# Attention projections of a two-layer float32 trunk: panels in pairs, four row tiles of each pair in seven block products, head norms scaled on ScalarE

## The chip, the cores and the metric

The kernel runs on one core of one Trainium2 chip. The metric is the device time of one execution in microseconds; the kernel before has a median of 2073.8 us over three runs.

## The reference

Everything is float32; 256 tokens, width 2048, 16 heads of 128, hidden width 8192, two layers. Cut to what matters:

```python
# layer a
u = rms_norm(h, a_norm_g)
q, k, v, fz = split(u @ a_w_in, [D, 2*D, 3*D])      # a_w_in: 2048 x (3*2048 + 16)
q, k = rms_norm per head (a_q_g, a_k_g)
logf = log_sigmoid(fz + a_b_f); c = cumsum(logf)
s = q k^T / sqrt(128) + c[query] - c[key], causal; p = softmax(s); o = p v
h = h + o @ a_w_out
h = h + relu(rms_norm(h, g) @ w1)**2 @ w2           # w1: 2048 x 8192
# shared keys and values, once
k_sh, v_sh = split(rms_norm(h, kv_norm_g) @ kv_w, [D]); k_sh = rms_norm per head
# layer b
q = rms_norm per head (rms_norm(h, b_norm_g) @ b_w_q)
s = q k_sh^T / sqrt(128) + relative-position bias, chunks of 64 masked; p = softmax(s)
h = h + (p v_sh) @ b_w_out
h = h + relu(rms_norm(h, g) @ w1)**2 @ w2
```

## The kernel before

**Products.** The 256 tokens are two blocks of 128 (`NB`), the width is 16 row tiles of 128 (`KT`). An output of 512 columns is a *panel*; its accumulators are two tiles of 128 x 512, one for each block of tokens. Activations lie on chip with the width on partitions, in two parts, `hi` and `lo`, and so does every weight tile while it is used; a float32 product is the sum of three passes, hi by hi, lo by hi, and hi by lo (`passes`, L525, L527, L529). Activations are the stationary operand, weights stream. A *unit* is a weight tile of 128 x 1024, that is two row tiles by 512 columns. A whole unit is 2 row tiles x 2 blocks x 3 passes = 12 matmuls of 512 columns.

**The stream of weights.** `units` lists all weight tiles of the program in the order of use. `load` starts the transfer of a unit on SP's queue (L245), `issue` splits it: ScalarE writes `hi` (L262), VectorE the rest `lo` (L263). `top_up` keeps two units ahead of PE split and three more loading. Everything else (norms, softmax, transposes, steps of the next stage) is cut into steps and put into `fill`, a list with one entry for each unit to come; `run_fill` issues one entry behind each unit. PE, VectorE, ScalarE and SP run their instructions in the order written; so the lists fix what stands behind what on each engine.

**Seven products.** The MLPs and the query projection of layer b already take panels in pairs. Over a couple of couples of row tiles a pair is a 2 x 2 by 2 x 2 block product: blocks of tokens by couples of row tiles, times couples of row tiles by panels. It is done with seven block products in place of eight. Their weight operands (`Form`) are the stored tiles "11", "21", "22" and sums of tiles, "T1" to "T4"; their activation operands are row tiles or prepared sums of them (`sums`, tiles `S`). In the narrow form (`cols` = 1024, the query projection) four row tiles are in the products, each product is one weight tile of 1024 columns and 6 matmuls, and the other twelve row tiles follow as whole units, six for each panel. The query projection's plan is

```python
"query": "a2 F b2 F a3 F b3 a4 b4 a5 a6 a7",
"": "a2 F a3 F a4 F a5 a6 a7 b2 b3 b4",
```

where `a` and `b` are whole units of the two panels and F a product; the first four products of a pair stand among the last whole units of the pair before, and `b5 b6 b7` among the first products of the next. `prepare` starts the loads of the tiles that are summed (`bring`, L866, on SP's queue) and makes the sums at fixed distances before the pair begins (the tables `UNITS`): T3 and T2 on VectorE (`make`, L882), T1 and T4 as DMAs of GpSimd's queue that add to a tile on chip (`put`, L888). In the loop of `mlp`, partial accumulators are combined on the way (ScalarE L970, L977, L995; VectorE L972, L983).

**The heads.** In both layers the projections of the heads run panel by panel in whole units: in layer a q, k, v of four heads, four times (twelve panels, with the gate product `gates`, L792, in between), in layer b k and v, four times (eight panels). `head_norm` squares an accumulator on ScalarE (L603), sums on VectorE (L606), adds and scales (L610), takes the power -1/2 on GpSimd (L611), multiplies all four heads by it in one VectorE instruction out of the accumulator (L615), transposes in blocks of 32 (L375), and a trip through DRAM (`carry`, L385 and L391) ends the transpose. `attend` puts the steps of `softmax` (scores on PE, L668 and L669, into a tile of the room `ps_s`; bias and maximum on VectorE, L678 to L682; exponential on ScalarE, L685) and of `values` (PE, L699 and L700, into a tile of `ps_o`; L702, L703) at fixed entries of `fill`.

**Accumulator rooms.** PSUM holds two pairs `acc0`, `acc1`, two tiles `ps_s` (scores, the gate product, and every second pair's second panel in the MLPs) and two tiles `ps_o` (values and small transposes).

**After the heads** the output projection runs with its first two panels in step and the others one after the other (`stage`), and its last three units run among the first products of the MLP.

Of the kernel before, what the change touches and what calls it, by code (L numbers as in the profile page):

```python
# [9 lines left out]
F32 = mybir.dt.float32  # L10
F32R = mybir.dt.float32r
AF = mybir.ActivationFunctionType
ALU = mybir.AluOpType
# [16 lines left out]
LAST = {"deep0": (4, 6, 5)}  # L30
ORDERS = {
# [7 lines left out]
}  # L39
UNITS = {  # L40
    "W1E": (25, 20, 9, 14, 11, 10),
    "W1I1": (9, 7, 5, 6, 4, 1),
    "W1F": (7, 5, 1, 5, 4, 3),
    "W1S": (8, 6, 4, 5, 4, 1),
    "W2F": (6, 5, 1, 5, 4, 3),
    "W2S": (7, 7, 4, 5, 3, 1),
    "W2L": (7, 5, 1, 5, 4, 2),
    "QF": (7, 6, 1, 3, 2, 1),
    "QS": (7, 5, 1, 5, 2, 2),
}  # L50
TURNS = (
    ((0, -1, 4, 5, 6, 6, 6, 7, 9),
     (0, -1, 3, 6, 7, 7, 7, 8, 8),
     (0, -1, 4, 7, 7, 7),
     (1, -1, 3, 4, 5, 5)),
    ((1, -1, 5, 14, 14, 14, 15, 20, 20),
     (0, 2, 8, 10, 10, 14, 18, 20, 22),
     (0, -1, 5, 6, 7, 7),
     (0, -1, 4, 5, 5, 5)),
)  # L60
# [21 lines left out]
def trunk(ctx: ExitStack, tc: tile.TileContext, xT, xr, gs, hg, bf, wgate, w_in, w_oa, w1a, w1fa, w1sa, w2fa, w2sa,  # L82
# [24 lines left out]
    def load_x(i):  # L107
        raw_x[i] = qkv.tile([P, DEEP], F32, name="xin", tag=("k0", "k1", "v0", "v1")[i], bufs=1)[:, : GH * T].rearrange("p (a t) -> p a t", a=GH)
        if i:
            SY.dma_start(raw_x[i], xT[:, i * GH : (i + 1) * GH, :])  # L110
# [22 lines left out]
    def queue(src, m):  # L133
        u = [src[i] for i in range(m)]
        n = KT // UA
        u[: 2 * n] = [u[i + q * n] for i in range(n) for q in range(2)]
        units.extend(u)
# [13 lines left out]
    class Pair:  # L151
# [3 lines left out]
        def __init__(self, big, src, order, third, units, wide=UN):  # L155
            self.big, self.src, self.third, self.units = big, src, third, units
            self.ps, self.t, self.adds, self.order = None, {}, order != "early", order
            self.deep, self.wide = wide == DEEP, wide > UN
# [5 lines left out]
        def plan(self, rest):  # L164
            made = [self.items(f"f{i} h{i}" if self.wide else f"f{i}") for i in range(7)]
            own = ORDERS[self.order].split()
            last = LAST.get(self.order, (4, 5, 6))
            plan = made[0] + rest[:1] + made[1] + rest[1:2] + made[2] + rest[2:] + made[3]
            n = 4
            for i in own:  # L170
                if i == "F":
                    plan += made[last[n - 4]]
                    n += 1
                else:
                    plan += self.items(i)
# [972 lines left out]
```

## Time and profile before

| what | value |
|---|---|
| median of three runs | 2073.8 us (2072.63 to 2076.03) |
| profiled execution, its own time | 2071.0 us |
| its span in the profile | 2068.8 us |
| busy: PE, VectorE, ScalarE, GpSimd | 2060.2, 1713.6, 1314.4, 223.9 us |
| DMA | 543.08 MB, mean 263 GB/s |

The span is the stretch of the profile from the first to the last instruction. Busy time is the time in which at least one instruction of the engine runs; consecutive matmuls overlap, so the price of one is read from the distance of two starts. PE and its weight loads (PEld) are shown apart.

### The profile page before, as it was taken

How to read it: one execution, taken by the hardware profiler on the slowest of the kernel's cores; microseconds unless marked ns; L12 is line 12 of the kernel's file. 1: busy time of each engine (PE TensorE's matmuls, PEld its weight loads, DVE VectorE, ACT ScalarE, POOL GpSimd, SP SyncE). 2: the span in 40 equal slices, each digit the busy share in tenths (PEclk: the TensorE clock that was granted, in tenths of full speed). 3: DMA queues.
4: the chain of work that ended last, by engine and by line, in shares of the span. 5: the costliest groups of instructions: out<-in, count | busy, mean ns of one | idle time of the engine just before them, and what ended most of it. 6: DMA issues, size and time to landing. Idle time of an engine off the chain costs nothing.

```text
span 2068.8 us, 26858 instructions
## 1 busy us (share of the span) xinstructions
PE 2060.2 (100%) x9140; PEld 1705.4 (82%) x9140; DVE 1713.6 (83%) x1974; ACT 1314.4 (64%) x1587; POOL 223.9 (11%) x339
## 2 busy tenths in 40 slices
PE   9999999999999999999999999999999999999999
PEld 8888888888888888888878888888788888888887
DVE  5767666899898899899988577778998988988996
ACT  6544444777677676677776445556766676776764
POOL 1111000021101102101011001000211111111020
PEclk9999999999999999999999999999999999999999
DMA  7777777788888898898878777777888888888985
GB/s 288 244 255 242 229 255 254 280 272 272 294 263 282 261 292 277 250 293 264 264 236 275 230 234 237 237 271 284 277 275 276 251 280 296 262 279 255 302 244 165
DMA packets 170682, 543.08 MB, mean 263 GB/s; under 512 B 40480, under 2 KB 68528, under 8 KB 147504
## 3 DMA queue, kind: packets, MB, share of 16 engines
q1 hardware_dynamic: 153008, 463.16, 62.7%
q0 software_dynamic: 17248, 77.64, 18.7%
q8 instruction: 72, 1.18, 0.2%
q14 instruction: 66, 0.54, 0.1%
q10 hardware_dynamic: 288, 0.57, 0.1%
HBM read 501.39 MB, written 26.24 MB: 255 GB/s over the span
## 4 chain that ended last, share of the span: by engine, by line
PE 98%; DMA 1%; ACT 0%; DVE 0%; POOL 0%; issue 0%; ACTq 0%; DVEq 0%; POOLq 0%
PE acc L529 26%; PE acc L525 26%; PE acc L527 26%; PE s L525 7%; PE s L529 7%; PE s L527 6%; PE s L669 1%; PE po L699 1%; DMA query<-turn 0%; PE s L668 0%; PE po L700 0%; DMA turn<-z 0%; DMA raw<-in_w_in 0%; PE s L792 0%; ACT hi L262 0%; POOL query L391 0%
## 5 line engine op out<-in xcount | busy, mean ns | idle before, releaser
L263 DVE TENSOR_TENSOR lo<-raw,hi 128x1024 fp32r<-128x1024 f32 (+1 forms) x461 | 555.9, 1211 | 164.7 <-ACT hi L262 151.9
L262 ACT ACTIVATE hi<-raw 128x1024 fp32r<-128x1024 f32 (+1 forms) x461 | 484.8, 1054 | 293.5 <-PE acc L527 228.2
L525 PE MATMUL acc<-hi,act 128*128 128x512 f32 x2076 | 578.9, 394 | 2.8 <-ACT hi L262 2.0
L529 PE MATMUL acc<-lo,act 128*128 128x512 f32 x2076 | 569.6, 389 | 0.1
L527 PE MATMUL acc<-hi,act 128*128 128x512 f32 x2076 | 569.4, 389 | 0.1
L527 PEld LDWEIGHTS acc<-hi,act 128*128 128x128 f32 x2076 | 389.9, 188 | 82.2 <-DVE act L356 0.5
L529 PEld LDWEIGHTS acc<-lo,act 128*128 128x128 f32 x2076 | 389.4, 188 | 82.4 <-DVE lo L263 1.6
L525 PEld LDWEIGHTS acc<-hi,act 128*128 128x128 f32 x2076 | 388.1, 188 | 82.4 <-ACT hi L262 2.8
L262 ACT ACTIVATE hi<-w 128x1024 fp32r<-128x1024 f32 x258 | 271.2, 1058 | 132.4 <-PE acc L527 111.2
L263 DVE TENSOR_TENSOR lo<-w,hi 128x1024 fp32r<-128x1024 f32 x258 | 309.9, 1217 | 16.5 <-ACT hi L262 15.3
L263 DVE TENSOR_TENSOR lo<-wT,hi 128x1024 fp32r<-128x1024 f32 x184 | 223.4, 1221 | 53.4 <-ACT hi L262 50.3
L262 ACT ACTIVATE hi<-wT 128x1024 fp32r<-128x1024 f32 x184 | 193.7, 1059 | 87.1 <-PE acc L527 35.9
L401 POOL DMA_DIRECT2D q<-z x208 | 103.6, 511 | 260.3 <-DVE z L375 210.3
L525 PE MATMUL s<-hi,act 128*128 128x512 f32 x358 | 98.4, 390 | 0.5 <-DVE s L983 0.5
L527 PE MATMUL s<-hi,act 128*128 128x512 f32 x358 | 98.2, 389 | 0.0
L529 PE MATMUL s<-lo,act 128*128 128x512 f32 x358 | 98.2, 389 | 0.0
L525 PEld LDWEIGHTS s<-hi,act 128*128 128x128 f32 x358 | 67.0, 188 | 14.6 <-issue 0.9
L527 PEld LDWEIGHTS s<-hi,act 128*128 128x128 f32 x358 | 67.2, 188 | 14.0
L529 PEld LDWEIGHTS s<-lo,act 128*128 128x128 f32 x358 | 67.2, 188 | 14.0
L882 DVE TENSOR_TENSOR wT<-wT,w 128x1024 f32<-128x1024 f32 x62 | 76.0, 1225 | 2.1
L262 ACT ACTIVATE hi<-zraw 128x1024 fp32r<-128x1024 f32 x53 | 56.0, 1056 | 30.9 <-PE acc L527 25.3
L882 DVE TENSOR_TENSOR wT<-w,w 128x1024 f32<-128x1024 f32 x62 | 75.3, 1214 | 0.3
(183 smaller groups left out, 1928.2 us busy)
## 6 DMA issues: line engine op xcount, KB each, us to landing
raw<-in_w_in SPq DMA_DIRECT2D x95, 512.0 KB, 4.5
w<-in_w2fa SPq DMA_DIRECT2D x32, 1024.0 KB, 6.8
raw<-in_w_kv SPq DMA_DIRECT2D x64, 512.0 KB, 4.5
w<-in_w2fb SPq DMA_DIRECT2D x32, 1024.0 KB, 6.6
w<-in_w1fa SPq DMA_DIRECT2D x28, 1024.0 KB, 7.3
w<-in_w1fb SPq DMA_DIRECT2D x28, 1024.0 KB, 6.8
raw<-in_w2sb SPq DMA_DIRECT2D x52, 512.0 KB, 6.6
raw<-in_w2sa SPq DMA_DIRECT2D x50, 512.0 KB, 6.8
```

Of the source, the lines that this page charges most:

```text
L262: S.activation(hi[:, c], raw[:, c], AF.Copy)
L263: V.tensor_tensor(lo[:, c], raw[:, c], hi[:, c].bitcast(F32), op=ALU.subtract)
L401: (G if i % 2 else SY).dma_start(dst[32 * j : 32 * j + 32, i * n : (i + 1) * n], z[32 * i : 32 * i + 32, j * n : (j + 1) * n])
L525: TE.matmul(ps[:, cols], xh, cut(hi, j), start=first, stop=False, **kw)
L527: TE.matmul(ps[:, cols], xl, cut(hi, j), start=False, stop=False, **kw)
L529: TE.matmul(ps[:, cols], xh, cut(lo, j), start=False, stop=last, **kw)
L669: TE.matmul(s[:, P : 3 * P], q[:, a, P:T], k[:, a], start=True, stop=True)
L699: TE.matmul(po[:, :T], v[:, 0, a * P : (a + 1) * P], pT[:, :2], start=True, stop=False)
L882: V.tensor_tensor(d, a, b, op=ALU.add)
```

## The change

**Heads in pairs.** The first pair of panels of each layer's heads stays in whole units; the panels behind it go in pairs in the narrow form: in layer a v0 with q1, k1 with v1, q2 with k2, v2 with q3, k3 with v3 (five pairs), in layer b k1 with v1, k2 with v2, k3 with v3 (three). Summed tiles lie in the second halves of the rooms of k and v (tiles `R` in the orders below) and in a tile of the activations' pool. The sums of x for the products are made in layer a from the first piece of x (`sum_x`), in layer b with the flipped activations. The loop of `mlp` becomes `run`, which both use; a mask (`HM`, `KM`) says how many entries of `fill` are issued behind each unit or product.

**Rooms.** Every second pair's second panel accumulates in `ps_s`, so scores and the gate product move to `ps_o`.

**Norms.** The scaling by the power of the mean square becomes four ScalarE activations of 128 columns with a scale per row, in place of one VectorE instruction, for all q and k panels. In layer b bias and maximum become one fused VectorE instruction.

**Output projections.** Panels 0 and 1 run in step to their sixth unit, then come two units of panel 2 (now in `ps_s`), the last two of panels 0 and 1, the rest of panel 2, and panel 3.

**Tables.** Entries of `fill` and distances are numbers in `TABLES`; many of those for the MLPs and the query projection change by a few places.

```diff
-        s = ps_s.tile([P, 512], F32, name="s")
+        s = ps_o.tile([P, 512], F32, name="po", tag="po")
...
+    "HF": (10, 8, 5, 7, 4, 3),
...
+    "XS": (0, 6, 5, 2),
...
+    def plan_heads(w, when):
+        pairs = []
+        for j in range(1, w.shape[0] // 16):
+            src = [[w[16 * j + 8 * q + u] for u in range(8)] for q in range(2)]
+            big = {k: src[int(k[1]) - 1][int(k[0]) - 1] for k in ("11", "12", "21", "22")}
+            pairs.append(Pair(big, src, "qkv" if when == "H" else "kv", j % 2 == 1, TABLES[when + ("F" if j == 1 else "S")]))
+            pairs[-1].at = 2 * j
+        tail = Tail(w, 8)
+        units.extend(w[i] for i in range(13))
+        return join(pairs, {"12": "k0", "22": "k1", "11": "v0", "21": "v1"}, tail), tail
...
             def turn():
                 qn = wk.tile([P, 512], F32, name="qn", tag="wk")
-                V.tensor_tensor(qn.rearrange("p (a d) -> p a d", a=GH), ps.rearrange("p (a d) -> p a d", a=GH),
-                                rn.unsqueeze(2).to_broadcast([P, GH, P]), op=ALU.mult)
+                for a in range(GH):
+                    c = slice(a * P, a * P + P)
+                    S.activation(qn[:, c], ps[:, c], AF.Copy, scale=rn[:, a : a + 1])
                 blocks32(qn, z, b)
...
             else:
-                V.tensor_tensor(t[:, c], s[:, c], bias[:, a, c], op=ALU.add)
-            V.tensor_reduce(nm[:, b : b + 1], t[:, c], axis=AX.X, op=ALU.max, negate=True)
+                V.tensor_tensor_reduce(out=t[:, c], in0=s[:, c], in1=bias[:, a, c], scale=-1.0, scalar=-3.0 * NEG,
+                                       op0=ALU.add, op1=ALU.min, accum_out=nm[:, b : b + 1])
...
+        p.t[name] = sub(p.rooms[name])[:, UN:] if p.order in ("qkv", "kv") else room(p.rooms[name], "w" + name)
...
+            elif p.order in ("qkv", "kv"):
+                t[name] = acts.tile([P, 2 * UN], F32, name="wT3", tag="act")[:, :UN]
...
+    def sum_x(fs):
+        y = raw_x[0]
+        for j in range(GH):
+            S.activation(y[:, j], y[:, j], AF.Copy, scale=gsb[:, j : j + 1])
+        yield
+        fs.extend(qkv.tile([P, UN], F32R, name="S", tag="S", bufs=2) for _ in range(2))
+        yield from sums([[y[:, j::2, b * P : (b + 1) * P] for j in range(2)] for b in range(NB)], fs)
...
+        evacs = [f(g) for g in range(NG) for f in (of_q, of_k, of_v)]
...
+        panels(x, evacs[1:2], None, after, tail=tail_h)
+        base = turns[0]
+
+        def open_pair(p):
+            p.ps, p.base = [None, acc_pair(2 if p.third else 1 - base)], base
+            p.x, p.fs, p.evac = x, fs, evacs[p.at : p.at + 2]
+
+        run(plan_h, open_pair, TABLES["HM"])
```

Three places show how instructions move. First PE in the heads of layer a, behind the first scores (before) and in the first pair (after). `s` in the second is an accumulator, `S` the sums of x, `acc` panel k0, whose last units stand among the products. Before:

```order
L668 MATMUL s<-k,q 128x128
L669 MATMUL s<-k,q 128x256
L525 MATMUL acc<-hi,act 128x512 x4
L527 MATMUL acc<-hi,act 128x512 x4
L529 MATMUL acc<-lo,act 128x512 x4
```

After:

```order
L553 MATMUL s<-hi,S 128x512 x2
L555 MATMUL s<-hi,S 128x512 x2
L557 MATMUL s<-lo,S 128x512 x2
L553 MATMUL acc<-hi,act 128x512 x4
L555 MATMUL acc<-hi,act 128x512 x4
L557 MATMUL acc<-lo,act 128x512 x4
```

A product has 6 matmuls for its weight tile where a whole unit has 12.

Second VectorE around the first q panel's norm in layer a, where the first pair now begins. `wT_416` is the summed weight tile T3 and then T2, `R` a stored tile of the sum, `sum` and `S` the sums of x, `ss` and `qn` belong to the norm. Before:

```order
L263 TENSOR_TENSOR lo<-raw,hi 128x1024
L610 TENSOR_SCALAR ss<-ss,ex 128x4 x2
L501 COPY rb<-rx 128x128 x2
L263 TENSOR_TENSOR lo<-raw,hi 128x1024
L615 TENSOR_TENSOR qn<-acc,ss 128x512
L375 STREAM_TRANSPOSE z<-qn 128x4x4x32
L505 COPY early<-pt 128x256
```

After:

```order
L287 TENSOR_TENSOR lo<-wT_416,hi 128x1024
L918 TENSOR_TENSOR wT_416<-wT_416,R 128x1024
L642 TENSOR_SCALAR ss<-ss,ex 128x4 x2
L401 STREAM_TRANSPOSE z<-qn 128x4x4x32
L529 COPY rb<-rx 128x128 x2
L366 TENSOR_TENSOR S<-sum,S 128x512 x2
L287 TENSOR_TENSOR lo<-raw,hi 128x1024
L401 STREAM_TRANSPOSE z<-qn 128x4x4x32
L533 COPY early<-pt 128x256
L287 TENSOR_TENSOR lo<-wT_416,hi 128x1024
```

The transpose of the scaled tile now follows the two small scalings with no split between, and the low halves of `S` stand behind it; the multiplication has left for ScalarE.

Third ScalarE in the second pair of the query projection of layer b, where it splits weights (`hi`), builds activations (`y`, `act`) and now scales (`qn`). Before:

```order
L262 ACTIVATE hi<-query 128x1024
L262 ACTIVATE hi<-raw 128x1024
L352 ACTIVATE y<-query,gsb 128x256 x2
L603 ACTIVATE sq<-s 128x512
L262 ACTIVATE hi<-w_9142 128x1024
L262 ACTIVATE hi<-raw 128x1024
L352 ACTIVATE y<-query,gsb 128x256 x2
L355 ACTIVATE act<-y 128x1024
L262 ACTIVATE hi<-raw 128x1024 x3
```

After:

```order
L378 ACTIVATE y<-q,gsb 128x256 x2
L381 ACTIVATE act<-y 128x1024
L649 ACTIVATE qn<-s,ss 128x128 x4
L286 ACTIVATE hi<-raw 128x1024 x2
L378 ACTIVATE y<-query,gsb 128x256 x2
L649 ACTIVATE qn<-s,ss 128x128 x4
L286 ACTIVATE hi<-raw 128x1024
```

Two groups of four scalings come in between the splits that PE takes next.

More of the change, by code (lines that the diff above doesn't have):

```diff
@@ L254, in issue @@
             form, half = raw, raw.half
+            assert form.name in form.pair.has, "unit early"
+            if form.name in ("T3", "T2"):
+                assert form.name + str(int(half)) in form.pair.has, "unit early"
+            form.pair.issued.add(form.name)
             raw, cuts = form.pair.t[form.name], [slice(0, form.pair.cols - UN if half else UN)]
@@ L881, in make @@
         d, a, b = (t[i][:, cols] for i in (name, a, b))
+        if name == "T3":
+            assert {"22", "12"} <= p.has and "T1" not in p.has, "T3 order"
+        if name == "T1":
+            assert "T30" in p.has and "T31" in p.has, ("T1 order", p.order, p.has, p.units, getattr(p, "at", 0))
+        for k in (0, 1):
+            if half in (None, k):
+                p.has.add(name + str(k))
+        p.has.add(name)
         V.tensor_tensor(d, a, b, op=ALU.add)
@@ L887, in put @@
         p.t[name] = p.t[at]
+        if name == "T1":
+            assert "T30" in p.has and "T31" in p.has, ("T1 order", p.order, p.has, p.units, getattr(p, "at", 0))
+        p.has.add(name)
         G.dma_start(p.t[name][:, : p.cols], p.big[other], accum_op=ALU.add)
@@ L997, in trunk @@
+    rooms.open()
+    o = heads()
     st1, x1, S1 = RowStats("m"), [], []
```

344 lines of the change are left out of this document (216 added, 128 removed), and 13 rows, old and new, of tables (ORDERS, TABLES).

## Prediction

> **What bounds the kernel now.** I read the page first: busy shares, clock, and the chain that ended last.
>
> ```profile
> span 2068.8 us, 26858 instructions
> ...
> PE 2060.2 (100%) x9140; PEld 1705.4 (82%) x9140; DVE 1713.6 (83%) x1974; ACT 1314.4 (64%) x1587; POOL 223.9 (11%) x339
> ...
> PE 98%; DMA 1%; ACT 0%; DVE 0%; POOL 0%; issue 0%; ACTq 0%; DVEq 0%; POOLq 0%
> ```
>
> TensorE (PE) runs from end to end and is 98% of the chain. Only 8.6 us of the span (2068.8 - 2060.2) have no matmul in them. Next came the table of stretches, cut at the stages: start, heads of layer a, output projection a, MLP a, the query projection, heads of layer b, output projection b, MLP b, tail. The columns are the stretch, its length, and busy time (instructions) of PE, PE's weight loads, VectorE, ScalarE and GpSimd, then clock, DMA share and GB/s.
>
> ```profile
> core 0: us, PE busy (x) PEld busy (x) DVE busy (x) ACT busy (x) POOL busy (x), PEclk, DMA share, GB/s
> ...
> 7.00:27.00 20.00, 19.98 (x81) 16.44 (x82) 16.17 (x25) 16.38 (x30) 0.00 (x0) 1.00 1.02 405
> 27.00:294.00 267.00, 267.00 (x1208) 221.97 (x1206) 181.80 (x284) 135.23 (x196) 31.47 (x30) 1.00 0.73 242
> ...
> 374.00:1050.00 676.00, 675.45 (x2976) 557.77 (x2975) 611.46 (x616) 471.70 (x518) 80.08 (x136) 1.00 0.86 273
> 1050.00:1104.00 54.00, 53.22 (x235) 43.35 (x234) 45.71 (x55) 41.09 (x57) 11.45 (x11) 1.00 0.78 246
> 1104.00:1316.00 212.00, 212.00 (x959) 176.50 (x958) 148.19 (x234) 108.00 (x159) 19.84 (x20) 1.00 0.76 247
> ...
> 1398.00:2064.00 666.00, 664.80 (x2933) 549.23 (x2932) 591.25 (x588) 451.58 (x479) 78.41 (x134) 1.00 0.84 267
> 2064.00:2068.80 4.80, 0.69 (x6) 0.49 (x5) 0.93 (x3) 0.00 (x0) 0.00 (x0) 0.98 0.31 109
> ```
>
> The heads, where the change works, keep PE busy without a gap (267.00 of 267.00, 212.00 of 212.00) while VectorE is at 68% and 70%. The MLPs, which already run in seven products, lose PE almost nothing with VectorE at 90% (611.46 of 676) and 89%. So in the heads time is the number of matmuls, as long as VectorE and ScalarE stay below what the MLPs bear. The waits of PE that a semaphore explains:
>
> ```profile
> PE acc L525 <- ACT hi L262: 2.0, 2, 1.1
> ...
> PE acc L525 <- ACT act L355: 0.7, 1, 0.7
> PE s L525 <- DVE s L983: 0.5, 1, 0.5
> ```
>
> They come to 3.2 us, none longer than 1.1 us; 0.9 of them is the first load.
>
> **The change, part by part.** *Fewer matmuls.* The price of one comes from the timeline of PE in the heads; a whole unit (12 matmuls) starts at 302.87 and its follower at 305.59:
>
> ```profile
> 302.87 1.07 PE L525 MATMUL acc<-hi,act 128*128 128x512 f32 x4
> 303.77 1.07 PE L527 MATMUL acc<-hi,act 128*128 128x512 f32 x4
> 304.68 1.07 PE L529 MATMUL acc<-lo,act 128*128 128x512 f32 x4
> 305.59 0.38 PE L668 MATMUL s<-k,q 128*128 128x128 f32 x2
> ...
> 1078.78 0.61 PE L525 MATMUL acc<-hi,S 128*128 128x512 f32 x2
> 1079.23 0.62 PE L527 MATMUL acc<-hi,S 128*128 128x512 f32 x2
> 1079.69 0.62 PE L529 MATMUL acc<-lo,S 128*128 128x512 f32 x2
> 1080.14 1.07 PE L525 MATMUL s<-hi,act 128*128 128x512 f32 x4
> ```
>
> 2.72 us for 12 is 0.2267 us each. The last four rows are from the query projection, which the kernel already does by the method that the heads now get: one of the seven products is 6 matmuls in 1.36 us, the same price. Two panels cost 2 x 8 x 12 = 192 matmuls before; a pair now has 12 whole units and seven products, 12 x 12 + 7 x 6 = 186. Eight pairs (five and three) drop 48, which is what the order of instructions shows (8826 matmuls of 512 columns become 8778): 48 x 0.2267 = **-10.9 us**. The output projections only reorder theirs, and the 64 matmul calls of scores and values stay.
>
> *More weight work.* The prices, from the groups by line (second last number: mean ns):
>
> ```profile
> L263 DVE TENSOR_TENSOR lo<-raw,hi 128x1024 fp32r<-128x1024 f32 x457 | 553.3, 1216 | 163.5 <-ACT hi L262 150.7 <-PE acc L527 9.3
> L262 ACT ACTIVATE hi<-raw 128x1024 fp32r<-128x1024 f32 x457 | 482.5, 1058 | 292.4 <-PE acc L527 228.2 <-PE s L527 29.2 <-ACT pbuf L685 9.7
> ...
> L882 DVE TENSOR_TENSOR wT<-w,w 128x1024 f32<-128x1024 f32 x62 | 75.3, 1214 | 0.3
> ...
> L615 DVE TENSOR_TENSOR qn<-acc,ss 128x512 f32<-128x512 f32 x30 | 20.4, 680 | 0.0
> ...
> L972 DVE SCALAR_TENSOR_TENSOR acc<-acc,p 128x512 f32<-128x512 f32 x17 | 11.7, 690 | 0.0
> ...
> L970 ACT ACTIVATE p<-acc 128x512 f32<-128x512 f32 x17 | 10.2, 599 | 14.4 <-PE acc L529 14.4
> ```
>
> A pair splits 19 weight tiles instead of 16: 3 x 1.22 us of VectorE, 3 x 1.06 of ScalarE. Two sums of weight tiles are VectorE's (2 x 1.21); the other two are accumulating DMAs. Two corrections of the accumulators cost VectorE 2 x 0.69 and three copies ScalarE at most 3 x 0.60. Per pair: VectorE +7.5 us, ScalarE +5.0. The scaling of q and k leaves VectorE (0.68 per tile, 16 tiles in the heads of a, 8 in those of b, 8 of the query projection). VectorE in the heads of a: 181.8 + 5 x 7.5 + 3 (sums of x) - 16 x 0.68 = 211 of 260 us, 81%; of b: 148.2 + 3 x 7.5 - 8 x 0.68 = 165 of 208, 79%. Both stay below the MLPs' 90%, so what covers this work is VectorE's own idle time: **0 us**. Without that cover a pair would cost up to 7.5 us.
>
> *The scaling on ScalarE.* 32 tiles become 4 activations of 128 columns each. The trace has none out of the accumulators with a scale per row; the nearest rows are wider:
>
> ```profile
> L352 ACT ACTIVATE y<-q,gsb 128x256 f32<-128x256 f32 x48 | 21.1, 494 | 1.9 <-DVE lo L263 1.9
> ...
> L724 ACT ACTIVATE v<-acc,rx 128x512 f32<-128x512 f32 x8 | 5.1, 686 | 8.5 <-PE acc L529 8.5
> ```
>
> From 512 to 256 columns the time falls by 192 ns, so by that slope another 96 ns to 0.40 us; in proportion to columns L724 gives 0.17. I take 0.40, since L352 is nearest in size. It is 128 x 0.40 = 51 us of ScalarE over the kernel. Heads of a: 135.2 + 5 x 5.0 + 64 x 0.40 + 3 = 189 of 260, 73%; heads of b: 108 + 3 x 5.0 + 32 x 0.40 = 136 of 208. The tight place is the query projection: 41.1 + 32 x 0.40 + 1.2 (sums) = 55.1 us of ScalarE in 54. Some of the 32 fall behind that stretch, so I price it at 1.0 us, between 0 and 2. [...]
>
> *Scores in layer b.* A sum and a maximum in two instructions become one fused instruction and a short read; the fused one is not in the trace. The maximum alone takes
>
> ```profile
> L682 DVE TENSOR_REDUCE row<-t 128x1 f32<-128x256 f32 x32 | 13.4, 420 | 1.1
> ```
>
> and less at 128 columns. If the fused form cost that much more than the two it replaces, 32 x 0.42 = 13 us would bring VectorE in the heads of b to 178 of 208, 86%; if it saved as much, to 73%. Either way 0 us.
>
> *The first pair.* VectorE's new order there is a chain: split of a summed tile 1.22, the next sum 1.21, two small scalings (L610), then it waits for GpSimd's power (L611) and for ScalarE's four pieces before a transpose, two small copies and the two low halves of the sums of x (L341), which the second product needs.
>
> ```profile
> 1076.34 0.23 DVE L610 TENSOR_SCALAR ss<-ss,eb 128x4 f32<-128x4 f32 x1
> ...
> L611 POOL TENSOR_TENSOR ss<-ss,mhalf 128x4 f32<-128x4 f32 x32 | 43.3, 1362 | 271.2 <-DVE ss L610 271.2
> ...
> L375 DVE STREAM_TRANSPOSE z<-qn 128x512 f32<-128x512 f32 x32 | 22.8, 712 | 1.1
> ...
> L341 DVE TENSOR_TENSOR S<-sum,S 128x512 fp32r<-128x512 f32 x10 | 6.4, 683 | 0.0
> ```
>
> With 1.36 + 4 x 0.40 for the wait, 2 x 0.23 for the scalings, 0.71, some 0.4 for the copies and 2 x 0.68 the chain is 8.3 us. PE meanwhile has the two gate groups (2 x 8 matmuls, 3.6 us), one product (1.36), one unit (2.72) and the first third of the second product (0.45): 8.1 us. I price **+1.0 us**, between 0 and 3. Before the change nobody waited there.
>
> *Start.* In 7 to 27 us the DMA engines are full (share 1.02, 405 GB/s), and three tiles of 0.5 MB for the first pair now enter SP's queue among the first loads, ahead of the last piece of x and of later weights. At that rate each holds up what is behind it by 1.3 us. PE lost 0.02 us there before, and behind it the share falls to 0.73: I take 0 us, at most 3 x 1.3 = 3.9.
>
> *Retimed rest.* The moved steps of MLPs and query projection may keep or lose the 2.3 us of waits above that are not the first load: I take -0.6, between -2.3 and +1 (another wait of the longest kind).
>
> *The sum.* -10.9 + 1.0 + 1.0 - 0.6 = -9.5 us. The profiled execution took 2071.0 us (its span of 2068.8 and 2.2 around it): 2061.5. The median of the runs shown is 2.8 higher, so **2064.3 us**.
>
> **The rivals.** *Slower: the room for scores.* The pairs need both tiles of the accumulator room that held the scores, so scores and values now share two tiles where they had two each. A matmul of values could then find its tile still being emptied:
>
> ```profile
> L703 DVE TENSOR_TENSOR act<-po,act 128x256 fp32r<-128x256 f32 x32 | 13.6, 425 | 50.5 <-ACT act L702 50.3
> ...
> L702 ACT ACTIVATE act<-po 128x256 fp32r<-128x256 f32 x32 | 12.3, 385 | 90.1 <-PE po L700 90.1
> ```
>
> ScalarE stood ready 90.1 / 32 = 2.8 us before each of the values tiles, so a tile is empty one copy and one subtraction after PE, 0.39 + 0.43 = 0.81 us. If each of 32 heads cost PE this once, 26 us return: 2064.3 + 26 = 2090.3, slower by 16.5. It decides from 10.9 / 32 = 0.34 us per head. Against it: scores and values of consecutive heads mostly stand several units apart in the new order.
>
> *Half the gain eaten.* The three bounds together, 3 us at the first pair, 2 in the query projection and 3.9 at the start, with 1 from retiming: 2073.8 - 10.9 + 9.9 = 2072.8; the largest two alone give 2073.8 - 10.9 + 6.9 = 2069.8.
>
> *The clock.* The first matmuls after the loads run at half rate:
>
> ```profile
> 7.01 1.22 PE L525 MATMUL acc<-hi,act 128*128 128x512 f32 x2 [0.90 <-ACT hi L262]
> 8.03 1.05 PE L527 MATMUL acc<-hi,act 128*128 128x512 f32 x2
> 8.89 1.05 PE L529 MATMUL acc<-lo,act 128*128 128x512 f32 x2
> ```
>
> Two of them take 0.86 us from 8.03 to 8.89, where two take 0.45 at 1078.78. If long waits brought this back, each would cost its own length and then matmuls at double price. For two waits of 3.5 us with 3.5 us of half rate behind them, 2 x (3.5 + 1.75) = 10.5 us: 2073.4, no gain. The 1.1 us waits of before show no such tail. [...]
>
> That the matmuls do not go is excluded by the order.
>
> **How the numbers follow.** Forecast (2060.6 to 2067): 0.72. Half eaten (2067 to 2073): 0.16, of which half is still over 0.2% faster; 0.2% is 4.1 us, about what a measurement of this kernel can tell from no change. The clock: 0.05, of which 0.03 with one such wait (about 2069, still faster) and 0.02 with two (no change). Slower by the scores' room: 0.07. Faster 0.72 + 0.08 + 0.03 = 0.83; same 0.08 + 0.02 = 0.10; slower 0.07. The low end has the 2.3 us of old waits gone and no new ones, 2073.8 - 13.2 = 2060.6; the high end takes in the largest two bounds, 2070.0; what lies outside is a little of the eaten case, the two long waits and the slower case, under 0.2.
>
> **What would show it.** Right: in the changed profile PE still above 99% of its span, the heads of a ending some 7 us sooner and those of b some 11 sooner, VectorE near 80% there, ScalarE fullest in the query projection. Wrong: new rows of waits of PE with more than 5 us in total; PE waiting at the scores or values line points to their room, at the second product of the first pair to the chain, at a split tile in the first 27 us to the loads, and matmuls at 0.43 us after a wait to the clock.

## The result and the profile after

The changed kernel takes 2066.6 us in the median of 11 runs, the kernel before 2072.0 in 11 runs beside them. The ratio is 0.9974, 95% interval [0.9965, 0.9984], so 5.4 us are gained, between 3.3 and 7.3. The prediction said 2064.3, in a range from 2060.6 to 2070.0, and reckoned with a gain of 9.5 us. The direction and the range hold; some two fifths of that gain are missing, and half of the 10.9 us of the matmuls. The rest of this text asks where they went. That the time is off by 2.3 us and the gain by 4.1 comes from the kernel before, whose median fell from 2073.8 us in three runs to 2072.0 in eleven. The profile of the changed kernel is of a run of 2064.5 us, the second shortest of the eleven.

First the head of the page of the changed kernel: span, busy time of the engines, and the chain that ended last.

```profile
span 2062.8 us, 26953 instructions
...
PE 2050.3 (99%) x9092; PEld 1694.5 (82%) x9092; DVE 1744.9 (85%) x2010; ACT 1380.6 (67%) x1771; POOL 224.6 (11%) x323
...
PE 91%; DVE 2%; DMA 1%; ACT 1%; issue 1%; SPq 0%; DVEq 0%; ACTq 0%; POOLq 0%
```

The 48 matmuls are gone (9140 to 9092) and PE is busy 9.9 us less, yet the span is only 6.0 us shorter (2068.8 to 2062.8). The part of the span without a matmul grew from 8.6 to 12.5 us, and the chain that ended last, which ran to 98% over PE, now leaves it for 9% of the way. In the page's line numbers of the changed kernel the three passes of a product are L553, L555 and L557, the splits of a weight tile L286 (ScalarE) and L287 (VectorE).

The table of stretches shows where PE lacks work (columns as in the prediction's table):

```profile
27.00:120.00 93.00, 90.18 (x401) 73.36 (x400) 73.25 (x113) 63.80 (x111) 15.28 (x15) 1.00 0.82 262
120.00:286.00 166.00, 166.00 (x753) 138.16 (x752) 133.72 (x194) 105.32 (x182) 26.41 (x25) 1.00 0.82 262
...
368.00:1042.00 674.00, 671.91 (x2958) 554.34 (x2958) 609.57 (x614) 472.54 (x518) 72.19 (x120) 1.00 0.87 273
...
1042.00:1096.00 54.00, 53.49 (x236) 43.61 (x235) 47.42 (x61) 41.70 (x64) 10.67 (x11) 1.00 0.87 268
...
1096.00:1305.00 209.00, 209.00 (x945) 173.96 (x944) 157.25 (x244) 136.78 (x239) 26.89 (x27) 1.00 0.82 262
```

The heads of b run without a gap, and so do those of a from 120 us on. In this trace the loss lies in the first groups of a (2.8 us of 93) and in the MLP of a (2.1 us of 674, where the kernel before lost 0.6 in its stretch). VectorE is as busy where PE never waits (133.72 of 166, 81%) as where it does (73.25 of 93, 79%): the share does not tell the two apart. The list of PE's waits names who was late:

```profile
PE acc L553 <- ACT hi L286: 4.5, 5, 1.2
PE s L557 <- DVE lo L287: 1.2, 3, 0.4
PE acc L553 <- ACT pbuf L719: 1.1, 1, 1.1
PE pt L126 <- DVE mhalf L128: 1.1, 1, 1.1
PE s L553 <- DVE s L968: 0.5, 1, 0.5
```

Without the 1.1 us at the very start (`pt`), which both kernels have, these waits sum to 7.3 us, where the kernel before had 3.2; the wait for the first load, 0.8 and 0.9, is in both sums. Those 4.1 us, and a slower matmul or two behind each wait (at 74.47 us four take 1.03 us, where four take 0.91 from 78.23 us on), are most of the 4.9 us that the spans of these two profiles miss. The same sum in two more profiles of the changed kernel (`again` and `again2` below) is 9.8 and 10.4 us. In the timeline each wait has a place. The largest five stand at 57, 74, 107, 439 and 1461 us (the last was there before, with 1.1 us, as were the 0.5 of L968); 464, 998 and 1486 have 0.4 each. In three of the new places a split stands on ScalarE behind an instruction that itself waits. At 74 us:

```profile
68.49 1.10 ACT L286 ACTIVATE hi<-wT 128x1024 fp32r<-128x1024 f32 x1
72.33 1.15 ACT L670 ACTIVATE q<-z,gqk 128x1024 f32<-128x1024 f32 x1 [2.73 <-DMA z<-turn]
73.38 1.99 ACT L286 ACTIVATE hi<-raw 128x1024 fp32r<-128x1024 f32 x2
...
74.47 1.19 PE L553 MATMUL acc<-hi,act 128*128 128x512 f32 x4 [1.19 <-ACT hi L286]
```

The scaling of the first group of q (L670) waits 2.73 us for its transposed tile; the next weight tile is split only after it, and PE waits 1.19 us. Its four transfers took 7.9 us to land, against 4.1 before. At 107 us it is the exponentials of a head (L719), which wait for VectorE's row maximum:

```profile
106.28 0.40 ACT L719 ACTIVATE pbuf<-t,row 128x128 f32<-128x128 f32 x1 [1.66 <-DVE row L713]
...
107.63 1.05 ACT L286 ACTIVATE hi<-raw 128x1024 fp32r<-128x1024 f32 x1
...
107.84 0.70 PE L553 MATMUL acc<-hi,S 128*128 128x512 f32 x2 [1.14 <-ACT pbuf L719]
```

At 57 us the gate's second copy stands ahead of the split:

```profile
56.10 0.37 ACT L842 ACTIVATE gz<-pg 16x256 f32<-16x256 f32 x1 [0.84 <-DVE gu L841]
...
57.47 1.19 PE L553 MATMUL acc<-hi,act 128*128 128x512 f32 x4 [0.49 <-ACT hi L286]
```

At 439 us, in the MLP of a, ScalarE has nothing to split, because a weight sum that GpSimd forms by an accumulating transfer lands late:

```profile
425.75 0.94 POOL L927 DMA_DIRECT2D wT<-in_w1fa  x1 [3.84 <-DVE lo L287]
...
439.24 0.73 PE L553 MATMUL acc<-hi,act 128*128 128x512 f32 x2 [1.21 <-ACT hi L286]
```

In the view of transfers (last number: us from issue to landing) it took 12.3 us, where the same one took 10.5 before:

```profile
wT<-in_w1fa POOLq DMA_DIRECT2D x1, 1024.0 KB, 12.3
```

In the runs below that have the same rows of times the wait grows with the landing. It is 0.25 us when the transfer takes 10.5 (`a_only`), 0.3 at 11.4 (`best`), 0.5 at 11.5 (`b_only`), 0.7 at 11.7 (`late_q`), 1.4 at 12.5 (`none`, `again2`) and 1.8 at 12.9 (`vnorm`).

At 464 us VectorE puts the low halves of the sums (L366) ahead of a split that PE needs:

```profile
462.05 1.29 DVE L366 TENSOR_TENSOR Sh<-sum,Sh 128x512 fp32r<-128x512 f32 x2
463.25 1.22 DVE L287 TENSOR_TENSOR lo<-wT,hi 128x1024 fp32r<-128x1024 f32 x1
...
464.52 0.74 PE L557 MATMUL s<-lo,Sh 128*128 128x512 f32 x2 [0.40 <-DVE lo L287]
```

### The profile page after: what moved, and what is told of

The parts are those of the page before. It is cut to its first block, busy times and chain, and to the rows that moved or that the text cites. A ratio compares the mean times of both kernels' runs of the same rounds, so it can differ in the third digit from the quotient of the medians.

```text
span 2062.8 us, 26953 instructions
## 1 busy us (share of the span) xinstructions
PE 2050.3 (99%) x9092; PEld 1694.5 (82%) x9092; DVE 1744.9 (85%) x2010; ACT 1380.6 (67%) x1771; POOL 224.6 (11%) x323
## 4 chain that ended last, share of the span: by engine, by line
PE 91%; DVE 2%; DMA 1%; ACT 1%; issue 1%; SPq 0%; DVEq 0%; ACTq 0%; POOLq 0%
PE acc L557 21%; PE acc L553 21%; PE acc L555 21%; PE s L557 9%; PE s L553 9%; PE s L555 9%; DVE lo L287 1%; PE po L739 1%; PE po L702 1%; DMA wT<-in_w1fa 1%; DMA raw<-in_w1a 0%; ACT hi L286 0%; PE po L740 0%; PE po L701 0%; DVE z L401 0%
## 5 line engine op out<-in xcount | busy, mean ns | idle before, releaser
L287 DVE TENSOR_TENSOR lo<-raw,hi 128x1024 fp32r<-128x1024 f32 (+1 forms) x428 | 517.6, 1215 | 118.0 <-ACT hi L286 106.9
L286 ACT ACTIVATE hi<-raw 128x1024 fp32r<-128x1024 f32 (+1 forms) x428 | 449.0, 1054 | 235.6 <-PE acc L555 159.3
L553 PE MATMUL acc<-hi,act 128*128 128x512 f32 (+1 forms) x1802 | 503.7, 393 | 4.5 <-ACT hi L286 4.5
L557 PE MATMUL acc<-lo,act 128*128 128x512 f32 (+1 forms) x1802 | 497.6, 389 | 0.1
L555 PE MATMUL acc<-hi,act 128*128 128x512 f32 (+1 forms) x1802 | 497.4, 389 | 0.0
L553 PEld LDWEIGHTS acc<-hi,act 128*128 128x128 f32 x1802 | 336.8, 188 | 75.5 <-ACT hi L286 6.5
L557 PEld LDWEIGHTS acc<-lo,act 128*128 128x128 f32 x1802 | 337.6, 188 | 72.1 <-DVE lo L287 2.1
L555 PEld LDWEIGHTS acc<-hi,act 128*128 128x128 f32 x1802 | 338.0, 188 | 71.1 <-DVE act L344 0.5
L286 ACT ACTIVATE hi<-w 128x1024 fp32r<-128x1024 f32 x258 | 271.6, 1059 | 125.7 <-PE acc L555 109.6
L287 DVE TENSOR_TENSOR lo<-w,hi 128x1024 fp32r<-128x1024 f32 x258 | 310.1, 1219 | 17.2 <-ACT hi L286 15.0
L287 DVE TENSOR_TENSOR lo<-wT,hi 128x1024 fp32r<-128x1024 f32 x208 | 252.4, 1221 | 60.5 <-ACT hi L286 56.5
L286 ACT ACTIVATE hi<-wT 128x1024 fp32r<-128x1024 f32 x208 | 219.6, 1060 | 98.4 <-PE acc L555 42.1
L553 PE MATMUL s<-hi,act 128*128 128x512 f32 x552 | 152.7, 393 | 0.5 <-DVE s L968 0.5
L557 PE MATMUL s<-lo,act 128*128 128x512 f32 x552 | 150.6, 389 | 0.4 <-DVE lo L287 0.4
L555 PE MATMUL s<-hi,act 128*128 128x512 f32 x552 | 150.6, 389 | 0.0
L557 PEld LDWEIGHTS s<-lo,act 128*128 128x128 f32 x552 | 103.5, 188 | 22.4 <-DVE lo L287 0.8
L555 PEld LDWEIGHTS s<-hi,act 128*128 128x128 f32 x552 | 103.6, 188 | 21.7
L553 PEld LDWEIGHTS s<-hi,act 128*128 128x128 f32 x552 | 102.9, 188 | 21.6 <-issue 0.9
L286 ACT ACTIVATE hi<-zraw 128x1024 fp32r<-128x1024 f32 x54 | 57.2, 1059 | 35.5 <-PE acc L555 26.4
L553 PE MATMUL acc<-hi,S 128*128 128x512 f32 x256 | 79.3, 391 | 1.1 <-ACT pbuf L719 1.1
L557 PE MATMUL acc<-lo,S 128*128 128x512 f32 x256 | 79.1, 390 | 0.0
```

Of the source, the lines that this page charges most:

```text
L286: S.activation(hi[:, c], raw[:, c], AF.Copy)
L287: V.tensor_tensor(lo[:, c], raw[:, c], hi[:, c].bitcast(F32), op=ALU.subtract)
L553: TE.matmul(ps[:, cols], xh, cut(hi, j), start=first, stop=False, **kw)
L555: TE.matmul(ps[:, cols], xl, cut(hi, j), start=False, stop=False, **kw)
L557: TE.matmul(ps[:, cols], xh, cut(lo, j), start=False, stop=last, **kw)
```

## Experiments

Theory A: the 48 matmuls bring their full 10.9 us, and new waits of PE at a few fixed places give a half of it back. The rivals stand in the expectations. There is one trace of each run, and one of the kernel before.

**The changed kernel again (again).** No edit.

> The changed kernel once more, as the measure for the others of this set. Theory A (a few waits): the missing 5 us are waits of TensorE fixed by the order of work, so they stand again in the trace at the same places: about 0.5 us near 57, 1.2 near 74, 1.1 near 107, 1.2 near 439, and the kernel is 5 to 6 us faster than before. Theory B (chance): the waits come from loads that land early or late by chance; then at least two of the four are gone or lie elsewhere, and others of the same sum stand in their place.

Ratio 0.9973 [0.9962, 0.9984], median 2067.2 of 12 runs against 2072.6. Between 40 and 120 us PE waits

```profile
PE acc L553 <- ACT pbuf L719: 1.1, 1, 1.1
PE acc L553 <- ACT hi L286: 0.7, 2, 0.5
```

and in the MLP of a again 1.2 and 0.4. So four of the five places repeat to a tenth of a microsecond, and the one at 74 us shrank to 0.2. But this trace also has waits that the first has not: 0.75 us at 1082 and, between 1380 and 1500 us, where the first has 1.1 us in all,

```profile
PE acc L557 <- DVE lo L287: 2.4, 2, 1.7
PE acc L553 <- ACT hi L286: 1.6, 1, 1.6
```

The 2.4 us stand at 1389 and 1393, at the end of the output projection of b. There ScalarE stood 3.96 us at the scaling of activations for a transfer (L378 at 1381.82), with two weight splits behind it, and PE then waited 1.66 us for VectorE's half of one. The pattern is that of 74 us. The second of these waits, 0.75 us, stands at that place in the traces of all runs below, with 0.7 or 0.8 us and also in `none`, so the first trace hides a loss that the new order brings. Theory A holds for waits set by the order of instructions (57, 107, 464); those that hang on a landing transfer vary, as theory B said of all, and the one at 439 is of this kind though it repeats here.

**Norms scaled on VectorE (vnorm).**

```
-                for a in range(GH):
-                    c = slice(a * P, a * P + P)
-                    S.activation(qn[:, c], ps[:, c], AF.Copy, scale=rn[:, a : a + 1])
+                V.tensor_tensor(qn.rearrange("p (a d) -> p a d", a=GH), ps.rearrange("p (a d) -> p a d", a=GH),
+                                rn.unsqueeze(2).to_broadcast([P, GH, P]), op=ALU.mult)
```

> The changed kernel with the 32 scalings of q and k tiles back on VectorE, one instruction each, and all else as changed. Theory A (waits by late transfers and by the order on ScalarE's queue): ScalarE loses 128 pieces of 0.29 us, VectorE gains 32 x 0.68 us, neither is the late one, so within 1.5 us of the changed kernel; the wait of 1.3 us at the second pair of the query projection, which stood before the change, may come back. Theory C (the pieces on ScalarE hold up the weight splits behind them): 3 to 5 us faster than the changed kernel, and the waits near 57, 74 and 107 us are gone.

2069.3 us, ratio 0.9980 [0.9969, 0.9991]: 2.0 us above the changed kernel of the same set, and not 3 to 5 below, nor within the 1.5 of theory A. The waits at 57 and 107 us stand:

```profile
PE acc L553 <- ACT pbuf L718: 1.1, 1, 1.1
PE acc L557 <- DVE lo L287: 0.8, 1, 0.8
PE acc L553 <- ACT hi L286: 0.5, 1, 0.5
```

Theory C falls. That putting the scaling back costs anything is not shown: the intervals overlap.

**Pairs in layer a alone (a_only), in layer b alone (b_only), in neither (none).** The edit for b's heads; the one for a's is alike, and `none` has both. Scores and values keep the shared room and get the old times.

```
-    plan_k, tail_k = plan_heads(w_kv, "K")
+    units.extend(w_kv[i] for i in range(w_kv.shape[0]))
...
-    o = heads_b()
+    o = [None] * H
+    for g in range(NG):
+        ...
+        panels(xkv, [head_norm(lambda: st2.flipped, zk, k)])
+        add_fill(attend(g, lambda g=g: qs[g], k, v, None, o, rel_bias))
+        panels(xkv, [v_evac(v, st2.flipped.r)])
```

> The changed kernel, but with the heads of layer b in whole units as before; the five pairs of layer a, the reordered output projections and the new times of the MLPs stay. 30 of the 48 matmul savings are left, 6.8 us. Theory A: 2.0 to 2.7 us less than the kernel before at the end of layer a's MLP after its waits, nothing won or lost in the heads of b: 1 to 3 us faster than before. Theory D (the loss is in layer b or after it): the whole 6.8 us and the heads of a end 6 us or more sooner.

> The changed kernel, but with the heads of layer a in whole units as before; the three pairs of layer b, the reordered output projections and the new times of the MLPs stay. 18 of the 48 matmul savings are left, 4.1 us. Theory A: all 4.1 us come in the heads of b, and the output projection and MLP of a still lose their 2 to 3 us beside the kernel before: 1 to 2 us faster than before. Theory D (the loss is in layer b or after it): no gain, or a loss. Together with the run that keeps layer a alone: by theory A the two gains add up to about 3 us with the MLP's loss counted twice, so to 5 to 6 with it counted once.

> The changed kernel with the heads of both layers in whole units as before. What is left of the change: the scaled norms on ScalarE, scores and values in one room, the fused instruction in the scores of layer b, the reordered output projections and the new times of the MLPs and the query projection. No matmul is saved. Theory A: the parts add up, so this is what the two kernels with one layer each leave, -2.8 - 0.7 + 5.4 = 1.9 us slower than before (1 to 3), with the waits at 437, 464, 1463 and 1490 us standing (shifted by some 2 us) and none in the heads. Rival (the other parts cost nothing, and the loss arises in the pairs): within 0.5 us of before.

Against before: `a_only` 0.9986 [0.9976, 0.9996], 2.8 us faster in the medians; `b_only` 0.9996 [0.9986, 1.0005], 0.7 us, not told from no change; `none` 1.0007 [0.9998, 1.0016], 1.5 us slower, again not told from no change. The 2.8 and the 1.5 fall where theory A put them, the 0.7 below its 1 to 2. Each of the two kernels with one layer has the cost of the rest in it, so the sum of both less that of `none` should be the whole change: -2.8 - 0.7 - 1.5 = -5.0, where -5.4 was measured. By these medians the pairs bring 6.5 us of the 10.9 (4.3 of 6.8 in a, 2.2 of 4.1 in b), and the rest of the change costs 1.5, with about 2 us of uncertainty on each. Neither theory D for layer b nor the rival of `none` is excluded by times alone. The trace of `none` says more than its time. Its heads of a lose nothing,

```profile
27.00:294.00 267.00, 267.00 (x1207) 221.98 (x1206) 173.84 (x269) 149.01 (x259) 32.14 (x30) 1.00 0.77 242
```

with the scaled norms and the shared room in them, and in its MLP of a PE waits between 400 and 500 us

```profile
PE acc L553 <- ACT hi L286: 1.4, 1, 1.4
PE s L557 <- DVE lo L287: 0.4, 1, 0.4
```

where the kernel before waited for nothing. `b_only` has none of the waits at 57, 74 and 107 us either, and `a_only` has those at 57 and 107: they belong to the pairs of layer a. Those at 439 and 464 belong to what `none` keeps of the change; that it is the new times of the MLP, and not the reordered output projections, is shown below for 464 alone.

**The first scaling of q four units later (late_q).**

```
-                    add_fill([[]] * (7 + (0 if g else 6)) + [[lambda: qs.update({g: scale_q(box[1], 0, g)})]])
+                    add_fill([[]] * (7 + (0 if g else 10)) + [[lambda: qs.update({g: scale_q(box[1], 0, g)})]])
```

> The scaling of the first group of q (ScalarE, which waits for its transposed tile to land) enters four units later, behind four more weight splits. Theory A (ScalarE's queue): the wait of TensorE near 74 us, 1.2, 0.4 and 1.0 us in three traces so far, is gone, and the others stay; TensorE reaches the unit at 80 us 0.4 to 1.2 us sooner. Rival: the splits there wait for their own loads, and a wait of 0.4 us or more stands within 10 us of the old place.

The splits now pass ahead of the scaling, and the matmuls run on:

```profile
78.60 1.06 ACT L286 ACTIVATE hi<-raw 128x1024 fp32r<-128x1024 f32 x1 [1.20 <-PE acc L555]
79.56 1.14 ACT L670 ACTIVATE q<-z,gqk 128x1024 f32<-128x1024 f32 x1
...
76.13 0.62 PE L557 MATMUL acc<-lo,act 128*128 128x512 f32 x2
76.59 1.07 PE L553 MATMUL acc<-hi,act 128*128 128x512 f32 x4
```

The wait is gone, as theory A said. That alone would prove little, since it is missing in `a_only` and `again2` too, where nothing was moved. It stands or falls with the landing of the four transfers: 1.2 us where they took 7.8 or 7.9 (`soft`, the first trace), 0.2 at 7.0 (`again`), 0.3 at 7.1 (`mlp_t0`), none at 6.6 (`a_only`) or 5.4 (`again2`). Here they took 7.6 us, and PE did not wait. The one run as a whole took 2068.8 us; its first unit started 1.5 us later (8.42 against 6.95 us), and its first dozen matmuls ran at half rate: at the last product ahead of that place PE is 3.47 us behind the first trace (75.23 against 71.76 us), 2.0 us more than at the start.

**The gate steps one unit later (gs2).** `"GS": (1,)` becomes `"GS": (2,)`.

> The gate steps of layer a enter one unit later. Theory A: the wait of 0.65 us near 57, which stood in all traces of this order, comes from ScalarE taking the second gate copy only when VectorE has added the first, ahead of the next split; one unit later the two stand elsewhere and the wait is gone or under 0.2 us. Rival (the stall is in the short products themselves, which leave 1.36 us for a split of 1.06 and one of 1.22): the 0.65 us stay.

Between 40 and 120 us:

```profile
PE acc L553 <- ACT hi L286: 0.3, 1, 0.3
PE acc L557 <- DVE lo L287: 0.2, 1, 0.2
PE pt L532 <- DVE rb L529: 0.2, 1, 0.2
```

beside the 1.1 us of L719. The wait at 57 us, 0.49 us in every other trace with the pairs of layer a, is gone: the gate steps were its cause, and not the short products by themselves. Three small ones stand in this trace, 0.7 us in all; whether the moved steps made them is not shown.

**The heads of the first group spread (soft).** The first row of `"ATA"`, `(11, 13, 15, 19, 10)`, becomes `(11, 14, 17, 20, 10)`.

> The four heads of the first group in layer a start 3 units apart (11, 14, 17, 20) and not at 11, 13, 15, 19. Theory A: the wait of 1.3 us near 107, the same in all traces of this order, comes from ScalarE standing at the exponentials of the third head until VectorE has its row maximum, with a split behind it; spread out, it is gone or under 0.4 us. Rival (the late load of a weight tile at 91 us pushes all behind it): a wait of 1 us or more stays between 95 and 115 us.

Of the waits in this stretch only the splits' are left, at 57 and 74 us:

```profile
PE acc L553 <- ACT hi L286: 1.7, 2, 1.2
```

The 1.1 us of L719 are gone, though the late weight tile at 91 us is still there (ScalarE waits 2.28 us for it, 2.29 before the move). All nine traces with the pairs of layer a and the old row have 1.1 to 1.2 us there, and the two with the new one nothing. Theory A.

**Old times in the MLP's first chunk (mlp_t0).** `"T0"` and `"W1I1"` get the values of `TURNS[0]` and `W1I1` before.

> The first chunk of both MLPs gets back two of its rows of times: when the hidden tiles are transposed and squared, and when the parts of the second pair of the first product are fetched. Theory A: the waits at 437 us (1.2 to 2.0) and at 464 (0.57, the same in all traces), and their twins at 1463 and 1490 in layer b, come from these rows: at 464 and 1490 they are gone, at 437 and 1463 down to what the kernel before had, 0.4 and 1.3; together 2 to 3 us less. Rival (they come from the weight loads, which the pairs of the heads shift): all four stay within 0.3 us.

The waits at 464 and 1490 are gone; those at 439 and 1463 are not. In layer a:

```profile
PE acc L553 <- ACT hi L286: 1.1, 1, 1.1
PE acc L553 <- ACT act L381: 0.8, 1, 0.8
PE acc L557 <- DVE lo L287: 0.6, 1, 0.6
```

More in sum than the 1.6 us of the changed kernel, but the 0.8 us (at 408) also stand in `hop_sh`, and 0.2 of them in `again2`, with other rows. Half right: the rows make the wait at 464; at 439 old rows in the new surroundings are not the old state, and the accumulating transfer took 13.1 us.

**Two moves in the same place (hop_sh).** The second row of `"T0"`, `(1, -1, 5, 6, 7, 8, 8, 9, 9)`, becomes `(2, -1, 5, 6, 7, 8, 8, 9, 10)`.

> Two moves in the first chunk of both MLPs: the 32 small transfers that turn the second hidden tile start one unit later, behind the next two loads of 1 MB in SyncE's queue, and VectorE forms the low halves of the sums of that tile behind the next split and not ahead of it. Theory A: the wait of 0.57 us at 464 and at 1490 (the split queued behind those low halves) is gone. For the wait at 437 and its twin at 1463, theory A1 (the accumulating transfer, 11.7 to 13.1 us against 10.5 before, shares the DMA engines with the 32 small ones): it lands in 11 us or less, and the wait falls below 0.5 us at 437. Rival A2 (it is slow because of the bytes in flight, whatever they are): the two loads of 1 MB now run beside it, it takes 13 us or more, and the wait grows past 1.5 us.

Both moves were wrong, 2073.5 us in the one run:

```profile
PE s L555 <- DVE Sh L366: 2.5, 1, 2.5
PE acc L553 <- ACT hi L286: 1.7, 1, 1.7
```

The low halves of the sums are needed at that very product, so behind the split they make PE wait 2.5 us for themselves. Nor is the accumulating transfer any quicker beside two loads of 1 MB, it takes 12.8 us: A1 is not borne out, though seven small transfers of GpSimd's queue still start during its flight (at 431.88), so it is not excluded. For A2 the wait is past 1.5 us, as it said, but the 12.8 lie among the 10.5 to 13.1 of the other runs: it is not shown either.

**Both helpful moves (best), and the changed kernel beside it (again2).** The edits of `late_q` and `soft`.

> The two moves that took a wait away without a new one of the same size: the first scaling of q four units later, and the four heads of the first group 3 units apart. Theory A: of the waits that came with the change 0.4 to 1.4 us at 74 and 1.3 us at 107 go, 0.4 us stay at 88: 1 to 2 us faster than the changed kernel of this set, so 6 to 8 us faster than before. Rival (TensorE's waits on the way are made up for later, or others of the same sum open): within 0.5 us of the changed kernel.

> The changed kernel beside the last one, on the same chip. By both theories 4.5 to 6.5 us faster than before; the waits near 57 and 107 us and at 464 and 1490 stand again with the same size, those at the first matmul, near 74, at 437 and 1463 with other sizes.

`best` 2065.8 us, 0.9973 [0.9964, 0.9983]; `again2` 2066.8, 0.9974 [0.9965, 0.9983]. In 40 to 120 us PE waits 0.8 us in `best`,

```profile
PE acc L553 <- ACT hi L286: 0.5, 1, 0.5
PE s L553 <- ACT hi L286: 0.3, 1, 0.3
```

and 2.5 in `again2`. The exponentials' 1.1 us are gone by the move; the move of the scaling had nothing to save here, since the four transfers took 5.1 us. The profiled run of `best` is the shortest of its nine (span 2061.3 us), so the spans are not compared. That the kernel is faster is not shown: 1.0 us between medians is inside the intervals. The places and sizes foreseen for `again2` are right (57, 107, 464 and 1490 as before, 74, 439 and 1463 changed).

## Why the prediction was right, and where it was not

- *Fewer matmuls, -10.9 us*: right in number (48) and price; the heads of b and those of a behind 120 us run without a gap.
- *More weight work, 0 us*: a step that failed. The loads were foreseen well (VectorE in the heads of a 207 of 259 us, 80%, said 81%; in b 157 of 209, 75%, said 79%), but the conclusion from a share below 90% to no cost was wrong. At 74 and 107 us PE lost 2.3 us to splits that stood on ScalarE behind a waiting instruction, and the term should have had a price and bounds for each instruction on ScalarE that waits for a transfer or for VectorE. Before the change ScalarE waited 3.3 us at the gate's second copy and up to 1.6 at a scaling of q in the same stage, and PE lost nothing. A product of 1.36 us leaves less time for such a wait than a whole unit of 2.72; that this is the difference is argued, not tested by itself.
- *The scaling on ScalarE*: 0.40 us a piece was too much.

```profile
L649 ACT ACTIVATE qn<-acc,ss 128x128 f32<-128x128 f32 x104 | 29.6, 376 | 7.8 <-POOL ss L643 7.7
```

One lasts 0.376 us, but four in a row overlap: 29.6 / 104 = 0.285 us of ScalarE each. The larger error is the place: only 8 of the 32 pieces run in the 54 us of the query projection (2.27 us, where 12.8 were added), so ScalarE is busy 41.7 us there and PE does not wait for it: the +1.0 should have been 0. Most of the others come behind it, and from 1096 to 1120 us ScalarE is busy 22.66 of 24 us while PE still has no gap.
- *The first pair, +1.0*: inside its bounds, for another reason. The second product does not wait,

```profile
51.28 0.71 PE L553 MATMUL s<-hi,S 128*128 128x512 f32 x2
```

its chain is quicker by the cheaper pieces (four take 1.14 us, said 1.60). The unit at 57 us does, 0.5 us behind the gate steps, which I had counted as work of PE alone.
- *Start, 0*: inside its bounds, but not nothing. Matmul for matmul PE is 0.9 us ahead of the kernel before at 55 us, only because the first matmuls in that trace of the kernel before ran at half rate: the 61st of 512 columns starts at 22.33 us there and at 20.69 here. Behind it 0.7 us are lost: eight matmuls from 23.49 to 25.95 us take 2.46 us and not 1.81, because the activations that they need (L343) stand on ScalarE behind a split that waited 1.60 us for its load. `b_only` and `none`, without the loads for the pairs of a, lose nothing there. In `again`, which starts at half rate too, nothing is lost either.
- *Retimed rest, -0.6*: wrong in sign, and the term that was mis-sized most. Against the kernel before, the waits of PE in the MLPs, the query projection and the output projections grew by 1.3 us in the first trace, by 4.9 in `again` and 4.0 in `again2`; the upper bound was 1. Most of that is at 439 us and between 1380 and 1500. In `none`, which has no pairs, they grew by 2.5, and its median is 1.5 us above the kernel before, between -0.4 and +3.3.
- *Scores in layer b, 0*: right. The fused instruction of 256 columns takes 0.42 us and its read 0.08, less than the sum (0.42) and maximum (0.42) of before.
- *The rivals*: no wait at a line of scores or values in the changed kernel, so the shared room costs nothing. "Half the gain eaten" is what came, mostly by other places than the three I named. That the time still fell into the forecast is partly luck: it lay 0.4 us below the border to that rival, and the ratio measured, applied to the 2073.8 us from which I reckoned, gives 2068.4, within the range but beyond the border. The sum for the clock took two waits of 3.5 us: no run shows one (the longest wait of PE is 3.2 us, in `late_q`). Half rate for 3.5 us does stand at the start of `before` (7.01 to 10.52 us), but where the clock fell behind a shorter wait it cost some 1.6 us on top (`gs2`), where the sum had 1.75.
- "New waits of more than 5 us" was the sign of being wrong. In sum PE waits 4.1 us longer than before in the first trace; but the waits at places where it did not wait before are 5.2 us there, 7.0 in `again` and 7.6 in `again2`. By that sign the time was right and the reading that VectorE's idle time and old distances cover the new work was not. The other sign says the same: in the output projections PE is 4.3 us (a) and 7.4 us (b) ahead of the kernel before, matmul for matmul, and not 7 and 11.

## What to carry to other kernels

Where one engine runs without a gap and the others are at 80%, the share says nothing on a shorter step (VectorE here: 81% where PE never waited, 79% where it did): look along the queue that feeds it for instructions that wait for something else, and see whether what stands behind them still arrives in time when the step is half as long. Move such an instruction behind the feed that it blocks and look for the wait that opens next. Read more than one trace of the same kernel before calling a place fixed: here the first one lacked a wait that nearly all others had. Two old rows put back into the retimed schedule took away one wait and not the other.

## What the runs showed of the chip

I had given the clock as a rival little weight, since waits of 1.1 us left no trace on it (granted clock 1.00 from 1466 to 1470 us in `before`, around one of them). Behind longer ones it did fall at times. In the trace with the gate steps moved PE waits 1.50 us in the MLP of b, and 2 us after it two matmuls take 0.85 us and not 0.45:

```profile
1464.07 0.73 PE L553 MATMUL acc<-hi,act 128*128 128x512 f32 x2 [1.50 <-ACT hi L286]
...
1466.21 1.05 PE L553 MATMUL acc<-hi,act 128*128 128x512 f32 x2
1467.06 1.06 PE L555 MATMUL acc<-hi,act 128*128 128x512 f32 x2
```

In the table of stretches the granted clock (third last column) is 0.58 there:

```profile
1466.00:1469.50 3.50, 3.50 (x10) 2.74 (x10) 2.93 (x4) 2.96 (x4) 0.00 (x0) 0.58 0.99 417
```

The same followed the wait there in `vnorm` (0.52), the run with the norms scaled on VectorE. In `again` a wait of the same place (1.6 us) was followed by the full clock:

```profile
1466.00:1469.50 3.50, 3.44 (x16) 2.48 (x15) 2.92 (x4) 3.50 (x6) 0.00 (x0) 1.00 0.88 351
```

From the start at the end of the wait to the second group of four (L555) it is 5.70 us in the one and 4.14 in `again`: some 1.6 us more (eight matmuls at 0.2 us above their price). The changed kernel itself has the same in `again2`, where a wait of 1.44 us at 440 us is followed by a granted clock of 0.52 from 442 to 445.5 us; in `hop_sh` it is 0.52 behind the wait of 2.53 us. After other waits as long the clock stayed full (`soft` 1.59 us and `best` 1.65, both with a mean granted clock of 1.000 over the span; `hop_sh` 2.21 near 1468, with a mean of 0.999 as in `gs2`, which has one fall). It fell to between 0.52 and 0.58 in four of thirteen traces, behind waits of 1.4 to 2.5 us and with PE otherwise at work. That the wait is the cause is argued from its place alone, and what decides between the two outcomes stays open. The rival "clock" of the prediction is thus not excluded: it is part of what single runs lose, by 1.6 us, though not in the first trace.

The first matmuls of the program ran at half rate in three of fourteen traces (`before`, `again`, `late_q`): in `before` two take 0.86 us from 8.03 us on, at a granted clock of 1.00, and in the first trace of the changed kernel 0.46 from 7.52. In `again` the 61st of 512 columns starts at 22.28 us, in the first trace of the same kernel at 20.69, so 1.6 us between two executions are decided there.

The accumulating transfer of 1 MB took 10.5 us before the change and 10.5 to 13.1 after it in the same place of the MLP. What makes it late was not found.
